# A hybrid attention and recurrence step on one core: pair products for the 32x32 diagonal blocks, the first norm on VectorE, window copies moved

## The chip, the cores and the metric

One core of a Trainium2 chip. The metric is the device time of one execution in microseconds (us). TensorE is PE here, its weight load PEld, VectorE DVE, ScalarE ACT, GpSimd POOL, SyncE SP (it only issues transfers).

## What is computed

One layer of a decoder trunk for a prompt of 2048 tokens and 32 sample tokens (8 sequences of 4): RMSNorm, one wide input projection, a sparse attention branch, a gated linear recurrence (HGRN2) of 4 heads with key and value width 128, merges, output projection, final norm. The recurrence is what the largest edit touches. Within a chunk, G is the running sum of the log gates, and query t takes key s with the factor exp(G[t] - G[s]), for s <= t only:

```python
def step(S, xs):
    qc, kc, vc, gc = xs
    G = jnp.cumsum(gc, axis=2)
    o_inter = jnp.einsum('bhtd,bhde->bhte', qc * jnp.exp(G), S)
    D = jnp.where(tri, G[:, :, :, None, :] - G[:, :, None, :, :], -jnp.inf)
    A = jnp.einsum('bhtd,bhtsd,bhsd->bhts', qc, jnp.exp(D), kc)
    o = o_inter + jnp.einsum('bhts,bhse->bhte', A, vc)
    ...
def rmsnorm(x, g):
    return x * rsqrt(mean(x * x, axis=-1) + EPS) * g
# outputs s_win_k, s_win_v: the sample's window buffers, the oldest 4 rows dropped, 4 new rows behind
```

## The kernel before

The program is written as generators, and the projections are fed as filling work beside the other stages: `load_x` (first norm) and then compression, sample attention, the recurrence (`hgrn`), the bias and setup of the prompt's attention, the prompt phase. A scheduler with a simulated timeline then sets the order in which each engine runs its instructions; it also orders what the engines issue to the DMA queues. So a step that is written in one place may run well before or behind it.

**First norm** (`load_x`, L287 to L326). 17 tiles of up to 128 rows by 1024. Each is loaded (L307, four buffers xt), multiplied by the gain on POOL (L309, xn), squared and summed on ACT (L312), its factor found by DVE in 128x1 steps (L313 to L320), xn scaled on DVE (L321), transposed on PE (L324), and split into a high and a low half (L325 on ACT, L326 on DVE). The projections' weights come in groups: loaded to `wraw` (one buffer, L270), their maximum on DVE (L277), a power-of-two scale (L188 to L193, with a transpose on PE), `us` (L280), and the split into wh (L283, ACT) and wl (L284, DVE). Projection products are L360, L420 and L439.

**Recurrence** (`hgrn`, from L574). 32 units of 256 tokens and one head, each of two pieces of 128 tokens. `factors` prepares one unit ahead: `common` makes G (L637), Bq, Bk, Xo and Kd; then for each level L of 64, 32, 16, 8, 4 the difference to the middle of each block of 2L (DVE, two halves, L679 and L680), its exponential (ACT, L681), and the products with keys and queries (POOL, L682 and L683). Each level so gives the scores between the first and second half of its blocks. `scores` sums them up per piece: a zero product (L697), the blocks of levels 64, 32, 16 into their places (L701), full 128x128 products for levels 8 and 4 (L703) and for pairs within four tokens (L704), each in a plane of a PSUM tile p; DVE then combines them under masks into AT (L706, L708 twice, L709). `values`, one unit later, takes AT and the state S to the outputs (L717 to L736). The 32 sample tokens (`sample_heads`) run beside the later units.

**Window copies** (`keep_windows`, L960 to L966): four DRAM to DRAM transfers of old window rows, written at the end of `sample_attention`. The loads of new window values there are L1179. Gathers of cached pages are issued by POOL (L839).

Of the kernel before, what the change touches and what calls it, by code (L numbers as in the profile page):

```python
# [23 lines left out]
D = 1024  # L24
# [29 lines left out]
def shape_constants():  # L54
# [56 lines left out]
    lm = np.zeros((128, 3, 128), np.float32)  # L111
    s, u = rows[:, None], rows[None, :]
    for i, L in enumerate((8, 4)):
        lm[:, i] = (s // (2 * L) == u // (2 * L)) & (s // L % 2 == 0) & (u // L % 2 == 1)
    lm[:, 2] = (s // 4 == u // 4) & (s <= u)
    c["lmask"] = lm.reshape(128, 384)
# [10 lines left out]
def trunk_kernel(ctx: ExitStack, tc: tile.TileContext, A, O):  # L127
# [120 lines left out]
    def make_projections(s2, st, sb):  # L248
# [38 lines left out]
        def load_x():  # L287
            with tc.tile_pool(name="xa", bufs=2, side="right") as xa, \
# [15 lines left out]
                for i, (t0, r) in enumerate(rows_of):  # L304
# [3 lines left out]
                    xn = xa.tile([128, D], F32, name="xn", bufs=3)  # L308
                    gp.tensor_mul(xn[:r], xt[:r], gB[:r])  # L309
# [11 lines left out]
                    ve.tensor_scalar(xn[:r], xn[:r], y, None, op0=OP.mult)  # L321
# [252 lines left out]
    def hgrn():  # L574
        with ExitStack() as st:
# [4 lines left out]
            lmf = hc.tile([128, 3, 128], F32, name="lmf")  # L580
            sy.dma_start(lmf, A["c_lmask"].rearrange("p (l t) -> p l t", l=3))
            lmi = hc.tile([128, 2, 128], I32, name="lmi")
            ve.tensor_copy(lmi, lmf[:, :2])
            zero = hc.tile([1, 128], BF, name="zero")
            ve.memset(zero, 0.0)
# [81 lines left out]
            def factors(c, h):  # L667
# [19 lines left out]
            def scores(u):  # L687
# [6 lines left out]
                for j in range(NJ):  # L694
                    tj = slice(j * 128, (j + 1) * 128)
                    p4 = pa.tile([128, 4, 128], F32, name="p4")
                    mm(p4[:, 0], zero, zero, True, False)  # L697
                    for li, L in enumerate(LEVELS[:3]):
                        X = u["Xs"][li][:, tj]
                        for s0 in range(0, 128, 2 * L):  # L700
                            mm(p4[s0:s0 + L, 0, s0 + L:s0 + 2 * L], X[:, s0:s0 + L], X[:, s0 + L:s0 + 2 * L], False, True)  # L701
                    for li in (3, 4):
                        mm(p4[:, li - 2], u["Xs"][li][:, tj], u["Xs"][li][:, tj], False, True)  # L703
                    mm(p4[:, 3], u["Bk"][:, tj], u["Bq"][:, tj], False, True)  # L704
                    AT = hp.tile([128, 128], F32, name="AT", bufs=4)
                    ve.tensor_mul(AT, p4[:, 3], lmf[:, 2])  # L706
# [1298 lines left out]
```

## Time and profile before

| | |
|---|---|
| median of 3 runs | 2533.16 us (2530.6 to 2539.71) |
| profiled execution | 2522.99 us |
| its span in the trace | 2521.0 us |
| busy: PE | 2381.2 us, 94% |
| busy: DVE, ACT, POOL | 64%, 45%, 41% |

The span runs from the first to the last instruction. A busy time is the sum of an engine's instruction durations, without overlap; matmuls are pipelined, so a busy PE is not necessarily at its peak. Times in the views below are from the span's start.

### The profile page before, as it was taken

Reading aid. Unit: us, or ns where it says so; the run is one execution under the profiler, and the core shown is the slowest. Engines: PE = TensorE matmul, PEld = TensorE weight load, DVE = VectorE, ACT = ScalarE, POOL = GpSimd, SP = SyncE. Lnnn points to the kernel's source line nnn. Section 1 sums busy time; section 2 is a strip of 40 time slices with the busy share of each in tenths; the row PEclk is TensorE's granted clock in tenths of the full one; section 3 lists DMA queues with packets and bytes.
Section 4 is the critical chain, followed back from the end, with each engine's and each line's share of the span. In section 5 each row is a group of like instructions: output and inputs, shape, how many; then the busy total and the mean of one; then the engine's idle time right before and its main releaser. Section 6 shows DMA issues by size and latency. Waiting matters only on the chain. (4 is left out here: it accounts for less than half of the span.)

```text
span 2521.0 us, 54571 instructions
## 1 busy us (share of the span) xinstructions
PE 2381.2 (94%) x21140; PEld 1589.5 (63%) x21140; DVE 1607.0 (64%) x4325; ACT 1122.3 (45%) x2287; POOL 1022.9 (41%) x1196
## 2 busy tenths in 40 slices
PE   5899999999999999999999879899999999999998
PEld 4788675555785566666666345657666666575765
DVE  8555554656325698777773667667777777867643
ACT  5434323421122344443442345536555656657663
POOL 4200102342111254434550004636566666677864
PEclk9999999999999999999999978999999999999999
DMA  7443315564322433333333552222222222211121
GB/s 275 139 140 112 123 68 164 191 226 153 125 69 100 143 119 115 114 100 109 93 101 96 182 161 65 72 85 72 72 57 74 53 70 55 61 54 44 46 60 45
DMA packets 266709, 264.87 MB, mean 105 GB/s; under 512 B 95101, under 2 KB 237873, under 8 KB 259281
## 3 DMA queue, kind: packets, MB, share of 16 engines
q1 hardware_dynamic: 257936, 223.62, 28.5%
q0 software_dynamic: 8512, 37.75, 4.6%
q8 instruction: 166, 2.72, 0.4%
q14 instruction: 95, 0.77, 0.1%
HBM read 181.90 MB, written 83.55 MB: 105 GB/s over the span
## 5 line engine op out<-in xcount | busy, mean ns | idle before, releaser
L1421 POOL TENSOR_TENSOR Pl<-P,Ph 128x512 f16<-128x512 f32 (+5 forms) x444 | 516.0, 1171 | 419.0 <-ACT Ph L1420 286.7
L1419 ACT ACTIVATE P<-st 128x512 f32<-128x512 f32 (+3 forms) x444 | 264.7, 596 | 207.1 <-PE st L1630 157.8
L360 PEld LDWEIGHTS <-wh 128*128 128x128 f16 x2240 | 214.8, 98 | 177.6 <-issue 28.3
L1420 ACT ACTIVATE Ph<-st 128x512 f16<-128x512 f32 (+5 forms) x444 | 263.3, 595 | 14.8 <-PE po L1428 9.9
L360 PE MATMUL ps<-xh,wh 128*128 128x512 f16 (+1 forms) x1120 | 231.9, 341 | 8.3 <-DVE row L373 8.0
L1508 DVE TENSOR_REDUCE mps<-mx 128x1 f32<-128x512 f32 (+3 forms) x320 | 188.3, 605 | 79.7 <-PE mx L1505 51.2
L360 PE MATMUL ps<-xh,wl 128*128 128x512 f16 (+1 forms) x1120 | 232.4, 340 | 0.0
L360 PE MATMUL ps<-xl,wh 128*128 128x512 f16 (+1 forms) x1120 | 230.3, 340 | 1.4 <-issue 1.4
L439 PE MATMUL ps<-wh,xh 128*128 128x256 f16 (+3 forms) x680 | 189.9, 279 | 5.3 <-ACT xh L325 4.1
L439 PE MATMUL ps<-wh,xl 128*128 128x256 f16 (+3 forms) x680 | 189.4, 278 | 2.1 <-DVE xl L326 2.1
L439 PE MATMUL ps<-wl,xh 128*128 128x256 f16 (+3 forms) x680 | 189.2, 278 | 0.0
L1427 PEld LDWEIGHTS <-Ph 128*128 128x128 f16 (+6 forms) x1776 | 139.2, 98 | 40.0 <-issue 5.0
L360 PEld LDWEIGHTS <-wl 128*128 128x128 f16 x1120 | 108.0, 98 | 85.4 <-issue 8.6
L439 PEld LDWEIGHTS <-xh 128*128 128x128 f16 (+1 forms) x1360 | 130.8, 99 | 29.9 <-issue 5.5
L1428 PEld LDWEIGHTS <-Ph 128*128 128x128 f16 (+6 forms) x1776 | 129.2, 96 | 32.0 <-issue 1.4
L1508 DVE TENSOR_REDUCE mpw<-mx 128x1 f32<-128x512 f32 (+3 forms) x224 | 104.3, 484 | 56.0 <-PE mx L1507 53.6
L682 POOL TENSOR_TENSOR X<-X,kt 128x128 f32<-128x128 f32 x160 | 78.1, 491 | 139.5 <-ACT X L681 139.3
L649 POOL TENSOR_TENSOR Xo<-Xo,qt 128x256 f32<-128x256 f32 x32 | 27.8, 869 | 259.7 <-ACT Xo L648 228.0
L1741 PEld LDWEIGHTS <-xh 128*128 128x128 f16 x1280 | 104.9, 98 | 32.0 <-issue 11.8
L1430 PEld LDWEIGHTS <-Pl 128*128 128x128 f16 (+3 forms) x1776 | 95.6, 97 | 30.8 <-POOL Pl L1421 8.0
L1505 PE MATMUL mx<-kas,qs 96*128 96x512 f16 (+3 forms) x320 | 108.2, 353 | 7.0 <-DVE mps L1508 5.2
L1428 PE MATMUL po<-vs,Ph 128*128 128x64 f16 x1088 | 107.6, 193 | 0.0
(539 smaller groups left out, 5974.8 us busy)
## 6 DMA issues: line engine op xcount, KB each, us to landing
wraw<-in_w_in_dram SPq DMA_DIRECT2D x22, 1024.0 KB
xt<-in_x_prompt_dram SPq DMA_DIRECT2D x32, 512.0 KB
ma_d<-row SPq DMA_DIRECT2D x8, 1040.0 KB
out_y_prompt_dram<-xt SPq DMA_DIRECT2D x16, 512.0 KB
sg<-ma_d SPq DMA_DIRECT2D x56, 128.0 KB
sg<-mb_d SPq DMA_DIRECT2D x56, 128.0 KB
mb_d<-row SPq DMA_DIRECT2D x18, 256.0 KB
q_d<-row SPq DMA_DIRECT2D x4, 1040.0 KB
```

Of the source, the lines that this page charges most:

```text
L360: mm(ps, l[:, kc], xs(r, t0, n)[:, kc], k == 0, k == 23)
L439: mm(ps, xs(l, t0, r)[:, kc], w[:, kc], k == 0, k == 23)
L682: gp.tensor_mul(Xv[:, :, :L], Xv[:, :, :L], kt.rearrange("p (b i) -> p b i", i=2 * L)[:, :, :L])
L1419: ac.activation(P[:n], ps, AF.Exp, scale=1.0 / QS)
L1420: ac.activation(ph[:n], ps, AF.Exp, scale=1.0 / QS)
L1421: sub.tensor_sub(pl[:n], P[:n], ph[:n])
L1427: mm(po[:, r, :w], ph[:n, rs[r]], v[:n, :w], first and r == 0, False)
L1428: mm(po[:, r, :64], ph[:n, rs[r]], v[:n, w:w + 64], False, False)
L1430: mm(po[:, r, :w], pl[:n, rs[r]], v[:n, :w], False, last)
L1505: mm(pmf[:, (x - ka) * 128:(y - ka) * 128], qq[:K, r], kk, i == 0, not sp_)
L1508: ve.tensor_reduce(mp_[:, r, c:c + 1], pmf[:, :n], axis=AX.X, op=OP.max)
L1741: mm(X["ps"], w[:, kc, cs], os_[o][:, kc], k == 0, k == 11)
```

## The change

- Scores: only the 64 pair and the two 32 pairs remain as blocks outside the 32x32 diagonal. The levels 16, 8, 4 and the pairs within four tokens are products of 32x32 for each of the four diagonal blocks. They lie in one 128x128 plane of PSUM, `near`, one 32-wide slot per kind. The zero product is gone.
- AT is one of four fixed tiles, zeroed once. ACT copies the 64 block and the two 32 blocks into it; DVE combines the four kinds in a 128x32 tile `own` (one product, three predicated copies), and one predicated copy over 128x128 puts `own` on the diagonal.
- Factors: one DVE subtraction over both halves, then the absolute value on ACT and the exponential with scale -1.
- First norm: the gain, the factor and the tile in one DVE step, POOL's multiplication is gone.
- The four window copies are issued behind the last load of window values.

```diff
-    for i, L in enumerate((8, 4)):
+    for i, L in enumerate((16, 8, 4)):
...
-    c["lmask"] = lm.reshape(128, 384)
+    own = np.repeat(rows[:, None] // 32 == np.arange(4)[None, :], 32, 1)
+    c["lmask"] = np.concatenate([lm.reshape(128, 128), own], 1).astype(np.float32)
...
-                    xn = xa.tile([128, D], F32, name="xn", bufs=3)
-                    gp.tensor_mul(xn[:r], xt[:r], gB[:r])
...
-                    ve.tensor_scalar(xn[:r], xn[:r], y, None, op0=OP.mult)
+                    xn = xa.tile([128, D], F32, name="xn", bufs=3)
+                    ve.scalar_tensor_tensor(xn[:r], xt[:r], y, gB[:r], op0=OP.mult, op1=OP.mult)
...
+            ATs = []
+            for i in range(4):
+                ATs.append(hc.tile([128, 4, 32], F32, name=f"AT{i}"))
+                ve.memset(ATs[i], 0.0)
...
-                    ref = Gv[:, :, L - 1:L].to_broadcast([128, nb, L])
+                    ref = Gv[:, :, L - 1:L].to_broadcast([128, nb, 2 * L])
...
-                    ve.tensor_tensor(Xv[:, :, :L], ref, Gv[:, :, :L], op=OP.subtract)
-                    ve.tensor_tensor(Xv[:, :, L:], Gv[:, :, L:], ref, op=OP.subtract)
-                    ac.activation(X, X, AF.Exp)
+                    ve.tensor_tensor(Xv, Gv, ref, op=OP.subtract)
+                    ac.activation(X, X, AF.Abs)
+                    ac.activation(X, X, AF.Exp, scale=-1.0)
...
-                    mm(p4[:, 0], zero, zero, True, False)
-                    for li, L in enumerate(LEVELS[:3]):
+                    near = p4[:, 1].rearrange("p (l t) -> p l t", l=4)
+                    for li, L in enumerate(LEVELS[:2]):
                         X = u["Xs"][li][:, tj]
                         for s0 in range(0, 128, 2 * L):
-                            mm(p4[s0:s0 + L, 0, s0 + L:s0 + 2 * L], X[:, s0:s0 + L], X[:, s0 + L:s0 + 2 * L], False, True)
-                    for li in (3, 4):
-                        mm(p4[:, li - 2], u["Xs"][li][:, tj], u["Xs"][li][:, tj], False, True)
-                    mm(p4[:, 3], u["Bk"][:, tj], u["Bq"][:, tj], False, True)
-                    AT = hp.tile([128, 128], F32, name="AT", bufs=4)
-                    ve.tensor_mul(AT, p4[:, 3], lmf[:, 2])
-                    for li in range(2):
-                        ve.copy_predicated(AT, lmi[:, li], p4[:, 1 + li])
-                    ve.tensor_add(AT, AT, p4[:, 0])
+                            mm(p4[s0:s0 + L, 0, s0 + L:s0 + 2 * L], X[:, s0:s0 + L], X[:, s0 + L:s0 + 2 * L], li == 0 or s0 == 64, True)
+                    for li, (l, r) in enumerate([(x, x) for x in u["Xs"][2:]] + [(u["Bk"], u["Bq"])]):
+                        for b in range(4):
+                            bs = slice(j * 128 + 32 * b, j * 128 + 32 * b + 32)
+                            mm(near[32 * b:32 * b + 32, li], l[:, bs], r[:, bs], li == 0 and b == 3, True)
+                    AT = ATs.pop(0)
+                    ATs.append(AT)
+                    ac.activation(AT[:64, 2:], p4[:64, 0, 64:].rearrange("p (b t) -> p b t", t=32), AF.Copy)
+                    for s0 in (0, 64):
+                        ac.activation(AT[s0:s0 + 32, s0 // 32 + 1], p4[s0:s0 + 32, 0, s0 + 32:s0 + 64], AF.Copy)
+                    own = hp.tile([128, 32], F32, name="own")
+                    ve.tensor_mul(own, near[:, 3], lmf[:, 3])
+                    for li in range(3):
+                        ve.copy_predicated(own, lmi[:, li], near[:, li])
+                    ve.copy_predicated(AT, lmi[:, 4:], own[:, None, :].to_broadcast([128, 4, 32]))
...
-                    sy.dma_start(vn, vd[2048 + 16 * gb:2064 + 16 * gb].rearrange("(b t) c -> t b c", t=4))
+                    X_last[0] = sy.dma_start(vn, vd[2048 + 16 * gb:2064 + 16 * gb].rearrange("(b t) c -> t b c", t=4))
...
-            keep_windows()
+            with tc.issue_after(X_last[0].ins):
+                keep_windows()
```

The rows below are engines' instructions in the order in which they run. On PE, the scores of one piece before (p is the PSUM tile, X a level's factors):

```order
L697 LDWEIGHTS zero
L697 MATMUL p_9902<-zero 128x128
L701 MATMUL p_9902<-X_9839 64x64
L701 MATMUL p_9902<-X_9845 32x32 x2
L701 MATMUL p_9902<-X_9851 16x16 x4
L703 MATMUL p_9902<-X_9857 128x128
L703 MATMUL p_9902<-X_9863 128x128
L704 MATMUL p_9902<-Bq,Bk 128x128
```

and with the change:

```order
L706 MATMUL p_9181<-X_9140 64x64
L706 MATMUL p_9181<-X_9146 32x32 x2
L710 MATMUL p_9181<-X_9152 32x32 x4
L710 MATMUL p_9181<-X_9158 32x32 x4
L710 MATMUL p_9181<-X_9164 32x32 x4
L710 MATMUL p_9181<-Bq,Bk 32x32 x4
L706 MATMUL p_9226<-X_9140 64x64
```

The zero product and the three 128x128 products are gone, sixteen products of 32x32 stand in their place, and the second piece follows at once.

On SP, at the start of the program before (the window copies among loads of x and weights):

```order
L966 DMA out_s_win_k_dram<-in_state_win_k_dram 16x4x4064
L307 DMA xt<-in_x_prompt_dram 128x1024
L270 DMA wraw<-in_w_in_dram 128x8x256
L966 DMA out_s_win_k_dram<-in_state_win_k_dram 16x4x4064
L966 DMA out_s_win_v_dram<-in_state_win_v_dram 16x4x4064
L307 DMA xt<-in_x_prompt_dram 128x1024
L966 DMA out_s_win_v_dram<-in_state_win_v_dram 16x4x4064
```

and with the change, in the middle of the program, where the sample attention ends:

```order
L1191 DMA vn<-vw_d 4x4x128
L978 DMA out_s_win_k_dram<-in_state_win_k_dram 16x4x4064 x2
L978 DMA out_s_win_v_dram<-in_state_win_v_dram 16x4x4064 x2
L400 DMA qb_d<-row 128x2080
L272 DMA wraw<-in_w_in_dram 128x8x256
L636 DMA lf<-lf_d 128x256
L637 DMA kt<-kb_d 128x256
```

The four now stand together behind the last load of window values, ahead of a store of projected rows, a weight load and the loads of the recurrence's first units.

## Rows read from the trace of the kernel before

**Rows 1.** The page's first part, busy time, share of the span and instructions.

```profile
PE 2381.2 (94%) x21140; PEld 1589.5 (63%) x21140; DVE 1607.0 (64%) x4325; ACT 1122.3 (45%) x2287; POOL 1022.9 (41%) x1196
```

**Rows 2.** Stretches of the recurrent stage: from and to, length in us, then the busy us and instructions of PE, PEld, DVE, ACT and POOL, the granted clock of PE, the DMA share and GB/s.

```profile
840.00:900.00 60.00, 59.33 (x441) 37.82 (x440) 52.79 (x133) 27.25 (x74) 27.90 (x48) 1.00 0.37 128
...
960.00:1020.00 60.00, 57.91 (x459) 38.83 (x457) 53.73 (x152) 27.31 (x77) 29.23 (x56) 0.99 0.36 119
1020.00:1080.00 60.00, 59.22 (x435) 38.88 (x435) 42.71 (x141) 23.64 (x71) 24.98 (x44) 1.00 0.33 99
...
1260.00:1320.00 60.00, 55.71 (x411) 36.09 (x409) 43.66 (x127) 24.91 (x75) 32.58 (x56) 0.97 0.31 101
```

**Rows 3.** Waits of PE from 840 to 1340 us: what waited, for what; us in total, times, longest us.

```profile
PE pu L781 <- DVE vm L779: 5.4, 3, 3.3
...
PE p L697 <- DVE AT L709: 2.9, 2, 2.5
...
PE pk L690 <- POOL Kd L655: 1.3, 2, 0.9
```

**Rows 4.** PE's timeline at one piece of scores: start us, length us, engine, line, operation, tiles, count.

```profile
928.12 0.23 PE L697 MATMUL p<-zero 1*128 1x128 bf16 x1
928.28 0.55 PE L701 MATMUL p<-X 128*64 128x64 f32 x14
928.76 0.71 PE L703 MATMUL p<-X 128*128 128x128 f32 x4
929.31 0.39 PE L704 MATMUL p<-Bq,Bk 128*128 128x128 f32 x2
929.63 0.23 PE L697 MATMUL p<-zero 1*128 1x128 bf16 x1
```

**Rows 5.** A stretch of L701 alone in the same piece: from and to, length, PE and PEld busy (instructions), clock, DMA share, GB/s.

```profile
928.53:928.66 0.13, 0.13 (x14) 0.13 (x12) 1.00 0.93 323
```

**Rows 6.** Two stretches of L1205 alone (the sample attention's products on four column strips), columns as in rows 5.

```profile
477.86:477.97 0.11, 0.11 (x4) 0.11 (x8) 1.00 0.09 37
477.83:478.65 0.82, 0.81 (x32) 0.81 (x32) 1.00 0.64 200
```

**Rows 7.** Groups of DVE instructions of the recurrence over the whole span: line, operation, tiles, shapes, count, then busy us, mean ns of one, idle us before them and what ended it.

```profile
L680 DVE TENSOR_TENSOR X<-G 128x128 f32<-128x128 f32 x160 | 67.3, 421 | 0.0
...
L679 DVE TENSOR_TENSOR X<-G 128x128 f32<-128x128 f32 x160 | 64.5, 403 | 34.6 <-PE p L701 25.8 <-PE p L703 8.8
...
L708 DVE COPY_PREDICATED AT<-lmi,p 128x128 f32<-128x128 int32 x128 | 34.0, 290 | 0.6
...
L706 DVE TENSOR_TENSOR AT<-p,lmf 128x128 f32<-128x128 f32 x64 | 17.8, 282 | 46.9 <-PE p L704 29.8 <-PE ov L721 17.1
L709 DVE TENSOR_TENSOR AT<-AT,p 128x128 f32<-128x128 f32 x64 | 17.2, 276 | 0.5
...
L652 DVE TENSOR_TENSOR E<-G 128x256 f32<-128x256 f32 x32 | 16.4, 512 | 0.0
```

**Rows 8.** Timeline of DVE, ACT and POOL around the same piece, columns as in rows 4; a length is that of all instructions of the row together (x5).

```profile
929.42 1.63 ACT L681 ACTIVATE X<-X 128x256 f32<-128x256 f32 x5
...
931.69 0.20 ACT L657 ACTIVATE eG<-G 128x2 f32<-128x2 f32 x1
...
931.98 0.17 DVE L751 TENSOR_TENSOR ATs<-pk,lmf 32x32 f32<-32x32 f32 x1
...
932.46 0.45 POOL L682 TENSOR_TENSOR X<-X,kt 128x128 f32<-128x128 f32 x1
```

**Rows 9.** Timeline of the start, columns as in rows 4; in brackets the idle us before it and what ended it.

```profile
9.09 6.95 POOL L309 TENSOR_TENSOR xn<-xt,gB 128x1024 f32<-128x1024 f32 x3 [7.73 <-DMA xt<-in_x_prompt_dram]
...
11.45 2.31 DVE L280 TENSOR_TENSOR us<-wxu,unx 128x1 f32<-128x1 f32 x1
...
13.86 2.19 DVE L320 SCALAR_TENSOR_TENSOR rsx<-rsx,rsz,sx 128x1 f32<-128x1 f32 x1
...
16.17 0.76 DVE L321 TENSOR_SCALAR xn<-xn,rsx 128x1024 f32<-128x1024 f32 x1
...
16.98 0.90 PE L324 MATMUL pt<-ident,xn 128*128 128x128 f32 x3 [5.95 <-DVE xn L321]
```

**Rows 10.** Waits of PE from 0 to 120 us, columns as in rows 3.

```profile
PE tp L183 <- DVE wmx L277: 8.9, 1, 8.9
PE pt L324 <- DVE xn L321: 5.9, 1, 5.9
```

**Rows 11.** Two more groups of DVE over the whole span, columns as in rows 7.

```profile
L1798 DVE SCALAR_TENSOR_TENSOR xt<-xt,rsq,fgB 128x1024 f32<-128x1024 f32 (+1 forms) x17 | 25.4, 1493 | 0.4
...
L326 DVE TENSOR_TENSOR xl<-pt,xh 128x1024 f16<-128x1024 f32 (+1 forms) x17 | 19.7, 1163 | 1.5 <-ACT xh L325 1.5
```

**Rows 12.** SP's queue at the start: start us and how long the issue held it.

```profile
23.41 2.60 SPq L966 DMA_DIRECT2D out_s_win_v_dram<-in_state_win_v_dram  x1
```

**Rows 13.** SP's queue and DVE where the window copies stand with the change, columns as in rows 9.

```profile
593.05 0.28 SPq L1179 DMA_DIRECT2D vn<-vw_d  x1
...
603.88 0.38 SPq L270 DMA_DIRECT2D wraw<-in_w_in_dram  x1
...
609.28 2.29 DVE L277 TENSOR_REDUCE wmx<-wraw 128x1 f32<-128x2048 f32 x1 [1.99 <-DMA wraw<-in_w_in_dram]
```

**Rows 14.** The first stretch of the span, columns as in rows 2.

```profile
0.00:60.00 60.00, 34.60 (x256) 28.22 (x257) 49.47 (x115) 31.61 (x57) 26.88 (x18) 0.97 0.78 270
```

More of the change, by code (lines that the diff above doesn't have):

```diff
@@ L110, in shape_constants @@
     c["edgeq"] = c["edge"].T.copy()
-    lm = np.zeros((128, 3, 128), np.float32)
-    s, u = rows[:, None], rows[None, :]
-    for i, L in enumerate((8, 4)):
+    lm = np.zeros((128, 4, 32), np.float32)
+    s, u = rows[:, None], rows[:, None] // 32 * 32 + np.arange(32)[None, :]
+    for i, L in enumerate((16, 8, 4)):
         lm[:, i] = (s // (2 * L) == u // (2 * L)) & (s // L % 2 == 0) & (u // L % 2 == 1)
-    lm[:, 2] = (s // 4 == u // 4) & (s <= u)
-    c["lmask"] = lm.reshape(128, 384)
+    lm[:, 3] = (s // 4 == u // 4) & (s <= u)
+    own = np.repeat(rows[:, None] // 32 == np.arange(4)[None, :], 32, 1)
+    c["lmask"] = np.concatenate([lm.reshape(128, 128), own], 1).astype(np.float32)
     rst = np.ones(2048, np.float32)
@@ L579, in hgrn @@
             po = st.enter_context(tc.tile_pool(name="hpo", bufs=1, space=PSUM, side="right"))
[L580 to L585, printed above, removed]
+            lmf = hc.tile([128, 8, 32], F32, name="lmf")
+            sy.dma_start(lmf, A["c_lmask"].rearrange("p (l t) -> p l t", l=8))
+            lmi = hc.tile([128, 8, 32], I32, name="lmi")
+            ve.tensor_copy(lmi, lmf)
+            ATs = []
+            for i in range(4):
+                ATs.append(hc.tile([128, 4, 32], F32, name=f"AT{i}"))
+                ve.memset(ATs[i], 0.0)
             rst = hc.tile([128, 256], F32, name="rst")
@@ L696, in scores @@
                     p4 = pa.tile([128, 4, 128], F32, name="p4")
[L697 to L698 removed]
+                    near = p4[:, 1].rearrange("p (l t) -> p l t", l=4)
+                    for li, L in enumerate(LEVELS[:2]):
                         X = u["Xs"][li][:, tj]
                         for s0 in range(0, 128, 2 * L):
[L701 to L709 removed]
+                            mm(p4[s0:s0 + L, 0, s0 + L:s0 + 2 * L], X[:, s0:s0 + L], X[:, s0 + L:s0 + 2 * L], li == 0 or s0 == 64, True)
[13 more added lines that the diff above has]
+                    ve.copy_predicated(AT, lmi[:, 4:], own[:, None, :].to_broadcast([128, 4, 32]))
+                    AT = AT.rearrange("p b t -> p (b t)")
                     u["AT"].append(AT)
@@ L750, in sample_heads @@
                     AT = hp.tile([32, 32], F32, name="ATs")
-                    ve.tensor_mul(AT, pb[:32, :32], lmf[:32, 2, :32])
+                    ve.tensor_mul(AT, pb[:32, :32], lmf[:32, 3])
                     yield
@@ L1218, in outputs @@
                                pT[:64, :128].rearrange("p (b h t) -> p h b t", h=8, t=4))
-            Xs = [{}, {}]
+            Xs, X_last = [{}, {}], [None]
             for _ in zip(compressed(0, Xs[0]), compressed(1, Xs[1])):
```

## The prediction, made before the changed kernel ran

> **What bounds the kernel now.** First the busy times of the whole span: TensorE (PE) is busy 2381.2 of 2521.0 us, 94% [rows 1], so time can come only from PE's work or from its idle rest of some 140 us. Next the stretches of the recurrent stage, where the largest edit lies: PE is busy 58 to 59 of each 60 us up to 1080 and still 55.7 near the end. VectorE (DVE) has 53 to 54 of 60 in the first third of the stage and 43 later; ScalarE (ACT) 24 to 27; GpSimd (POOL) 25 to 33 [rows 2]. Then PE's waits there: in 500 us the largest group is 5.4 us in three waits, the finished scores AT held PE for 2.9 and POOL's Kd for 1.3 [rows 3]. So little feeds PE too late there; a microsecond taken from PE's own instructions in this stage is a microsecond of the end, as long as the feeders keep up.
>
> **Scores, what is removed.** The timeline of one 128-token piece: the zero product starts at 928.12, the next piece's zero product at 929.63, so a piece costs PE 1.50 us. Of this the 64, 32 and 16 level blocks (L701) run to 928.76, and three full 128x128 products (L703 twice, L704) take from there to about 929.6 [rows 4].
>
> **Scores, what comes in.** One 64x64 pair stays: L701's first stretch, from 928.28 to where its small blocks begin, 0.26 us [rows 4, 5]. Behind it come two 32x32 pairs and four kinds of four 32x32 blocks, 18 products, 36 matmuls as f32 counts them, on four column strips of 32. What does one of these cost? Two rows bear on it. The four-strip product of the sample attention (L1205) starts four matmuls of 128 columns in 0.11 us, and 32 of them last 0.82 us [rows 6]: 26 ns a matmul of 128 columns, so the four strips work side by side. With 32 columns in place of 128, a round of four is 0.11 x 32/128 = 0.027 us; 36 matmuls in ten rounds are 0.27 us. And L701's own small blocks, on strips too, are 12 of the 14 matmuls in the 0.13 us behind the pair, 11 ns each [rows 5], which for 36 gives 0.40. With the 64 pair and an allowance of 0.10 for the change of tile sizes a piece is 0.63 by the one and 0.76 by the other; I take 0.70 between them, since both rows are near in kind and neither has these tiles. Saved: 0.80 us x 64 pieces = **51 us**. Ends: 0.63 gives 56, 0.76 gives 47; and were each 32-column matmul to cost the 26 ns of L1205's mean, a piece would be 0.26 + 0.94 + 0.10 = 1.30 and the gain 13 (rival 1).
>
> **What the scores and factors ask of the feeders.** DVE per unit (two pieces; 32 units): ten halves of 128x128 at 0.40 to 0.42 become five of 128x256 at 0.51 (L652's form), which saves 1.5 us; the evacuation per piece was 0.28 + 2 x 0.29 + 0.28 = 1.14 [rows 7] and becomes four of 128x32, priced at the 0.17 of a 32x32 product [rows 8], and one predicated 128x128 at 0.29: 0.97. So DVE loses 1.9 us a unit, 60 in all. ACT gets a second activation at each level, 160 x 0.33 = 53 us (five exponentials in 1.63 us), and six copies a unit, 192 x 0.20 = 38 us, at the price of a small one [rows 8]: 91 us over some 500, which takes it from 25 of 60 to about 36. That is free only as cover by PE's work and ACT's idle time; without the cover it is rival 3. POOL's products stay, 0.45 each [rows 8]. With a tenth less PE time in the stage, DVE's 53.5 of 60 in 840 to 1020 would be full [rows 2], were it not for the 1.9 us a unit that it loses. I take back a third of the 16 us that this third of the stage saves: **+5** (0 to +25).
>
> **First norm.** At the start POOL multiplies three tiles by the gain, 6.95 us for three, before DVE can scale the first; the first transposes begin at 16.98 after a wait of 5.95 us. Meanwhile DVE's 128x1 steps take 2.31 and 2.19 us [rows 9], where a 32x32 step takes 0.17 elsewhere [rows 8]: they stand beside POOL's multiplication. Without it I take these two at 0.2 each, 4.1 us earlier. Against that the fused step costs more than the old scaling. Its nearest row is the final norm's same operation, 1.49 us on average [rows 11], against 0.76 [rows 9]; in an undisturbed place I take 1.2, the 1.16 of a two-operand step of that size [rows 11], so +0.44. The transposes would begin near 13.3. In the first 120 us PE waits 8.9 us once for the weight maximum and 5.9 in one wait for the first norm [rows 10]; the second is what shrinks. I take **-5** for the start, with some for the later tiles. Ends: -14, if the 8.9 goes down with it by as much, and +3, if the fused step is 0.7 dearer and the scaling of four tiles stands on the path. What is late next is the weight maximum.
>
> **Windows.** Four copies of 1016 KB leave the start, where the longest of the four issues holds the queue for 2.60 us [rows 12] and the memory is at 270 GB/s [rows 14], and are issued behind the last load of window values (593.05). Next on that queue stands a weight load, at 603.88, whose reduction already waited 1.99 us for it [rows 13]. The four move 4.1 MB, at 270 GB/s [rows 14] 15 us of all DMA engines. If the weights came 15 us later, DVE would stand still at the reduction and with it the evictions behind it. The weight buffer is single, but weights are loaded and split ahead of their use, which leaves PE with work. I take **+2** (0 to +6, at worst 15), and no more gain at the start than counted, as no first wait of PE there ends on a transfer [rows 10].
>
> **Sum.** -51 + 5 - 5 + 2 = -49. The profiled execution took 2522.99 us (span 2521.0), so 2474 on its scale. The median of the runs shown, 2533.16, is 10 above; on that scale **2484**. This case's own range: 2468 to 2500 (all ends together 2463 to 2519).
>
> **Rivals.**
> 1. *The 32x32 products run one after another*, 26 ns each: -13 - 5 + 2, and nothing given back: **2517**. For it: L1205's mean is 26 ns, and nothing there shows that fewer columns would make it less. Against it: 11 ns each in L701 [rows 5, 6]. Chance 0.10. The Trainium skill has this as a rule: "TensorE: Matmul & The Clock Gate", section "Wait — 56ns, not 53.3ns?", says that starts of consecutive matmuls are never nearer than about 25 ns, however few the columns. L701's stretch disagrees with it for products on different strips; by the rule a piece would be 1.30 and the kernel this rival.
> 2. *The evacuation paces the stage.* DVE at 53.5 of 60 has no room for a faster PE in the first third [rows 2], and the shorter pieces ask for their evacuations closer together; half of the 51 comes back as waits for AT and for the projections' evictions: -26 - 5 + 2, **2505**. Against it: DVE gets 60 us less to do, it is at 43 later, and PE waited for AT only 2.9 us [rows 2, 3]. Chance 0.12. The Trainium skill warns of this in "TensorEngine Tiling (Array Packing)", section "PSUM Bottleneck": after array packing the copy out of PSUM can become the limit and both engines should share it, which this change does in part.
> 3. *Slower: the unit's own chain becomes what PE waits for.* Subtract, Abs, exponential, product follow one another level by level, and five Abs at 0.33 and six copies at 0.20 lengthen it by 2.85 us a unit. If ACT holds the levels back, PE stands at the scores, the 51 saved lies idle, and 32 x 2.85 = 91 is added: 2533 + 91 - 3 = **2621**. It decides as soon as POOL's last product of a unit comes less than 2.85 us ahead of its scores. Against it: units are prepared ahead, PE's waits for POOL there are 1.3 us [rows 3], and POOL at 0.9 a level is slower than ACT at 0.66 [rows 8], so that POOL paces the levels anyway. Chance 0.04.
>
> That the whole order of work moves, so that something outside these places eats the rest (ends near no change), gets 0.06.
>
> **How the numbers follow.** The forecast has 0.68. A measurement of this kernel tells about 0.5%, 12.7 us, from no change, so faster means below 2520.5. The forecast, rival 2, and six tenths of rival 1 lie there: 0.68 + 0.12 + 0.06 and a point of the remainder, 0.87. Within 0.5%: the rest of rival 1 and most of the remainder, 0.08. Slower: rival 3 and a point, 0.05. The range, 2460 to 2517, holds the forecast but for its tails (0.63), rival 2 (0.12) and about half of rival 1 (0.05).
>
> **What the profile of the changed kernel would show.** A piece between two 64x64 pairs in PE's timeline at 0.65 to 0.75 us (1.3 would be rival 1). PE still busy 56 or more of each 60 us in the recurrent stage, and its last values product 45 to 50 us earlier than before (far more waits for AT: rival 2; waits for POOL's X or ACT at the scores: rival 3). First transposes near 13 us, and the 128x1 steps of DVE there under 0.3 us. The window copies near 590 us and the next weight reduction later by at most their 15 us, with few us of PE idle behind it. The prediction is wrong if the pieces are short but PE's idle in the stage has grown by as much.

## The result, and the profile after

The changed kernel takes **2499.28 us** (median of 4 runs, 2497.57 to 2502.58), the kernel before 2534.85 beside it: a ratio of 0.9859, 95% interval 0.9838 to 0.988, or 36 us. Forecast were 2484, 49 us less than before, in a range of 2460 to 2517.

The first line of its page: PE is as full as before, with 1088 matmuls more.

```profile
PE 2357.9 (94%) x22228; PEld 1554.0 (62%) x22228; DVE 1575.8 (63%) x4232; ACT 1198.0 (48%) x2639; POOL 989.9 (40%) x1179
```

To say where the time went, the span is cut at two places that both kernels have: the first product of the recurrent stage's scores on PE (the transposes of Kd), and the first product of the prompt phase (L1620 before, L1633 after). Rows are as in [rows 2]: from and to, length, PE busy and so on. Before:

```profile
0.00:627.90 627.90, 580.66 (x4318) 406.63 (x4319) 367.12 (x830) 233.87 (x367) 140.67 (x125) 0.99 0.49 159
627.90:1493.80 865.90, 828.32 (x5898) 536.26 (x5896) 546.43 (x1545) 303.87 (x775) 257.59 (x455) 0.98 0.36 115
1493.80:2511.10 1017.30, 972.26 (x10928) 646.63 (x10926) 689.01 (x1938) 583.82 (x1145) 624.66 (x618) 0.97 0.23 63
```

and after:

```profile
0.00:628.70 628.70, 586.54 (x4339) 408.37 (x4340) 359.71 (x843) 240.31 (x387) 106.42 (x118) 0.99 0.49 160
628.70:1469.80 841.10, 798.04 (x6965) 498.67 (x6963) 519.86 (x1437) 371.68 (x1105) 258.13 (x445) 0.97 0.37 117
1469.80:2486.10 1016.30, 973.33 (x10927) 646.96 (x10926) 691.74 (x1938) 585.32 (x1146) 625.35 (x618) 0.97 0.23 64
```

The whole difference of the two traces, 25 us, lies in the middle stretch: 865.9 to 841.1. There PE's busy time fell by 30 us, and what it stood idle (length less busy) grew from 37.6 to 43.1. The median differs by 11 us more than the traces, and the granted clock shows why: the profiled execution of before ran at a mean of 0.980, its timed runs at 0.971 to 0.979 (one of 2543.12 us at 0.971, one of 2525.1 at 0.978), the changed kernel's at 0.973 to 0.976. So the trace of before shows an execution some 12 us shorter than the median; in which stretch those 12 us would lie is not known.

**The scores.** PE's timeline of two unbroken pieces after:

```profile
859.11 0.48 PE L706 MATMUL p<-X 128*64 128x64 f32 x4
859.39 0.23 PE L710 MATMUL p<-X 128*32 128x32 f32 x2
859.42 0.20 PE L706 MATMUL p<-X 128*32 128x32 f32 x2
859.44 0.34 PE L710 MATMUL p<-X 128*32 128x32 f32 x20
...
859.64 0.26 PE L710 MATMUL p<-Bq,Bk 128*32 128x32 f32 x7
859.83 0.48 PE L706 MATMUL p<-X 128*64 128x64 f32 x4
...
860.54 0.71 PE L729 MATMUL pu<-v,kd 128*128 128x128 f32 x4
```

A piece is 0.72 us (859.11 to 859.83), where [rows 4] had 1.50: 20 matmuls of 32 columns begin between 859.44 and 859.60.

**The waits of PE** in the middle stretch of the changed kernel (us, times, longest):

```profile
PE pu L793 <- DVE own L717: 6.0, 3, 2.6
PE ov L614 <- DVE o_sb L611: 5.3, 5, 1.6
PE ps L421 <- ACT piece L426: 5.0, 3, 2.5
PE ps L361 <- DVE row L383: 4.8, 3, 3.8
PE pk L694 <- POOL Kd L658: 3.7, 4, 2.0
...
PE p L710 <- POOL X L687: 1.1, 3, 0.6
```

Three of the five largest, 16 us, end on VectorE, each of another line, which points at its queue more than at one operation. For the finished factors (POOL's X, the last row) PE waits 1.1 us only. In 840 to 960 VectorE has 54.5 and 54.4 of 60, as full as in [rows 2] although a unit asks some 1 us less of it; that PE now asks sooner would explain it:

```profile
840.00:900.00 60.00, 54.06 (x559) 33.28 (x559) 54.52 (x138) 35.95 (x118) 33.46 (x56) 0.97 0.38 127
900.00:960.00 60.00, 57.17 (x630) 35.48 (x628) 54.39 (x147) 35.77 (x126) 34.43 (x59) 1.00 0.42 137
```

**The clock behind a wait.** The longest of the waits at L793, and the stretch around it (rows as in [rows 2]):

```profile
1077.52 1.19 PE L793 MATMUL pu<-vm,kd_s 32*128 32x512 f32 x1 [2.61 <-DVE own L717]
```

```profile
1066.80:1077.00 10.20, 8.11 (x108) 4.19 (x105) 8.70 (x27) 8.11 (x32) 8.15 (x16) 1.00 0.51 172
1077.00:1083.90 6.90, 6.38 (x13) 2.13 (x14) 3.79 (x19) 0.94 (x6) 3.18 (x8) 0.51 0.33 99
1083.90:1090.00 6.10, 6.10 (x99) 3.42 (x96) 1.05 (x5) 1.91 (x9) 0.04 (x1) 1.00 0.40 110
```

PE waited 2.61 us, and then the granted clock was 0.51, that is 1.2 GHz, for 6.9 us: the wait cost itself and some 3 us more. Such stretches add to 27.1 us in the middle stretch of before and to 44.6 after. In the recurrent stage of the changed kernel there are seven, each beginning within 4 us of a wait of 1.2 to 3.8 us; four other waits of 1.4 to 1.8 us brought none. The 17.5 us more of slow clock in the middle stretch are 9 us of PE's work.

### The profile page after: what moved, and what is told of

It reads as the page before. It is cut to its first block, busy times and chain, and to the rows that moved or that the text cites. A ratio compares the mean times of both kernels' runs of the same rounds, so it can differ in the third digit from the quotient of the medians.

```text
span 2496.1 us, 57172 instructions
## 1 busy us (share of the span) xinstructions
PE 2357.9 (94%) x22228; PEld 1554.0 (62%) x22228; DVE 1575.8 (63%) x4232; ACT 1198.0 (48%) x2639; POOL 989.9 (40%) x1179
## 4 chain that ended last, share of the span: by engine, by line
PE 68%; DVE 14%; DMA 7%; ACT 4%; issue 4%; POOL 1%; SPq 1%; DVEq 0%; ACTq 0%; POOLq 0%
PE ps L361 14%; PE ps L440 9%; PE ps L1786 7%; PE ps L1754 6%; PE ps L421 4%; PE st L1643 3%; PE st L1633 3%; PE mx L1518 3%; DVE X L683 2%; DMA wraw<-in_w_in_dram 2%; PE ph L920 2%; PE po L1440 2%; PE po L1443 2%; PE po L1441 2%; DVE mps L1521 1%
## 5 line engine op out<-in xcount | busy, mean ns | idle before, releaser
L361 PE MATMUL ps<-xl,wh 128*128 128x512 f16 (+1 forms) x1120 | 236.0, 347 | 1.1 <-issue 1.0
L1440 PEld LDWEIGHTS <-Ph 128*128 128x128 f16 (+5 forms) x1776 | 138.8, 98 | 41.3 <-issue 6.9
L1441 PEld LDWEIGHTS <-Ph 128*128 128x128 f16 (+5 forms) x1776 | 128.7, 96 | 32.7 <-issue 1.4
L1521 DVE TENSOR_REDUCE mpw<-mx 128x1 f32<-128x512 f32 (+3 forms) x224 | 104.9, 485 | 49.6 <-PE mx L1520 46.7
L652 POOL TENSOR_TENSOR Xo<-Xo,qt 128x256 f32<-128x256 f32 x32 | 30.5, 953 | 260.4 <-ACT Xo L651 229.3
L1518 PE MATMUL mx<-kas,qs 96*128 96x512 f16 (+3 forms) x320 | 109.8, 355 | 10.4 <-DVE mps L1521 7.7
L1440 PE MATMUL po<-vs,Ph 128*128 128x65 f16 x1088 | 106.6, 192 | 0.8 <-DVE otmp L1535 0.8
```

Source lines behind the costliest of these rows:

```text
L361: mm(ps, l[:, kc], xs(r, t0, n)[:, kc], k == 0, k == 23)
L1440: mm(po[:, r, :w], ph[:n, rs[r]], v[:n, :w], first and r == 0, False)
L1441: mm(po[:, r, :64], ph[:n, rs[r]], v[:n, w:w + 64], False, False)
L1518: mm(pmf[:, (x - ka) * 128:(y - ka) * 128], qq[:K, r], kk, i == 0, not sp_)
L1521: ve.tensor_reduce(mp_[:, r, c:c + 1], pmf[:, :n], axis=AX.X, op=OP.max)
```

## Experiments

Each was timed in several rounds against the kernel before on the same chip, which took a median of 2532.61 to 2535.96 us there. The three stretches are cut as above, one trace for each kernel; idle is PE's, and slow is the sum of the stretches at half clock, both of the profiled execution.

| kernel | median us | ratio to before [95%] | first stretch | middle: length, idle, slow | prompt: length, idle, slow |
|---|---|---|---|---|---|
| before | 2534.85 | 1 | 627.9 | 865.9, 37.6, 27.1 | 1017.3, 45.0, 51.4 |
| the change | 2499.28 | 0.9859 [0.9838, 0.988] | 628.7 | 841.1, 43.1, 44.6 | 1016.3, 43.0, 64.6 |
| scores_only | 2503.71 | 0.987 [0.9847, 0.9893] | 623.2 | 844.7, 42.0, 58.0 | 1025.8, 47.0, 51.2 |
| factors_only | 2506.67 | 0.9893 [0.987, 0.9917] | 628.9 | 849.7, 21.5, 24.7 | 1016.7, 42.1, 50.4 |
| norm_only | 2536.07 | 1.0009 [0.9993, 1.0025] | 621.3 | 872.5, 41.7, 35.0 | 1032.8, 52.6, 70.9 |
| windows_only | 2539.7 | 1.0025 [1.0011, 1.0039] | 638.2 | 859.1, 35.8, 29.3 | 1026.5, 48.4, 59.4 |
| products_twice | 2491.1 | 0.9825 [0.9806, 0.9844] | 624.9 | 833.6, 29.4, 23.9 | 1020.6, 42.8, 37.5 |
| vm_pool | 2514.88 | 0.9922 [0.9901, 0.9942] | 625.1 | 841.6, 47.2, 44.8 | 1035.1, 55.2, 74.7 |
| halves_exp | 2504.5 | 0.9882 [0.9863, 0.9901] | 625.8 | 845.6, 43.1, 61.4 | 1023.1, 47.3, 54.6 |
| windows_early | 2517.92 | 0.9938 [0.992, 0.9955] | 619.7 | 860.1, 50.1, 64.4 | 1027.6, 52.4, 68.7 |
| last_level_first | 2489.53 | 0.983 [0.9806, 0.9854] | 621.5 | 835.1, 39.8, 42.1 | 1015.1, 43.3, 46.7 |
| scores_factors | 2527.2 | 0.9975 [0.9961, 0.9988] | 620.0 | 849.4, 47.1, 43.8 | 1041.3, 55.5, 89.3 |
| no_subtract | 2467.28 | 0.9737 [0.9712, 0.9763] | 633.7 | 806.3, 29.0, 44.4 | 1026.2, 43.0, 51.2 |
| less_vector | 2470.93 | 0.9754 [0.9729, 0.978] | 616.3 | 828.7, 30.5, 34.1 | 1023.5, 44.6, 51.2 |

### One part at a time

The first four take one part of the change each into the kernel before; the edit is that part of the diff, so it is not shown again.

**scores_only.** 

> Only the scores and their masks change; factors, first norm and windows are as before. Theory A (the scores are the whole gain of the stage, what is lost of it goes to waits of PE on VectorE and to the clock behind them): ratio 0.987 to 0.990, 25 to 33 us faster, the two pieces of a unit in 1.4 to 1.6 us where nothing stands between them, PE waits of 840 to 1340 above the 18.8 us of before. Theory B (the sum of the prediction holds and the run-to-run spread hides it): 0.980 to 0.983, over 43 us faster. Theory C (the gain needs the shorter VectorE work of the factors as well): under 15 us.

Measured 0.987, 32 us: Theory A, at its edge, and by its signs too: two pieces with nothing between them take 1.41 to 1.48 us, and PE's waits from 840 to 1340 are 29.3 us. PE's products of the scores, counted as under products_twice below, fall from 99.1 us to 57.1.

**norm_only.** 

> Only the first norm changes. Theory A: first transposes 3.5 us earlier, of which 2 to 4 us arrive at the end: ratio 0.998 to 0.999. Rival: the later tiles' waits take it back, 1.000 +- 0.001.

Measured 1.0009 with 1 inside the interval: the rival. The first transposes came 3.9 us earlier (13.04), but the first product of the compression, behind all tiles of x, came 0.8 us later than before. The first stretch as a whole ends 6.6 us sooner with the same 4318 matmuls, but it differs by as much between kernels that share this part of the program, and the stretches behind it are 22 us longer.

**windows_only.** 

> Only the four window copies move. Theory A: the weight reduction behind them waits 2 us longer, PE waits near 600 us 0 to 3 us more, nothing is won at the start: ratio 0.999 to 1.002. Rival: the start's loads come earlier and PE's waits of the first 120 us shrink by some us: 0.997 to 0.999.

Measured 1.0025, 6 us slower, above Theory A's range (the interval reaches into it). The first stretch is 10 us longer, the middle one 7 shorter. DVE's weight reduction behind the copies waited 4.09 us for its weights, [rows 13] having 1.99.

**factors_only.** 

> Only the factors change: one subtraction, Abs, exponential. Theory A: VectorE gets about 1.5 us a unit less to do by the prediction, but the subtraction's mean in the changed kernel is 631 ns where 512 were assumed and PE is the bound: ratio 0.998 to 1.002. Rival (VectorE paces the first third of the stage): 0.994 to 0.997. Rival 3 of the prediction (Abs lengthens the chain): above 1.003.

Measured 0.9893, 27 us faster: the rival, and more than it asked for. Not one product was taken from PE. Its middle stretch shows what changed: PE busy is the 828 us of before, in 16 us less.

```profile
628.90:1478.60 849.70, 828.19 (x5900) 534.03 (x5898) 525.38 (x1392) 348.89 (x931) 266.03 (x456) 0.99 0.37 118
```

The idle time fell from 37.6 to 21.5, PE's waits on VectorE in this stretch from 21.0 to 5.6, VectorE's busy time by 21. So in the kernel before VectorE held PE back, by a few late arrivals that were read as too little to matter; one trace on each side shows it, and the order of work moved as well. By their ratios the four parts add to -33 - 27 + 2 + 6 = -52 us, and together they give 36.

The granted clocks of the timed runs say where most of the 16 us between lie. One minus the granted clock, times the span, estimates what half clock cost a run (too much where PE had nothing to do in it). On average it is 49 us in factors_only, where the kernel before had 65 beside it; 61 in scores_only, 67 in norm_only, 71 in windows_only; 64 in the change, where the kernel before had 63. So the clock is 13 us of the parts' 52 and nothing of the change's 36. Without it the parts add to 38 and the change gives 36: what is lost when the parts stand together is mostly clock.

### Both large parts, and what each of the others is worth beside them

**scores_factors.** Without the first norm's and the windows' part.

> Scores and factors change, the first norm and the window copies stay as before. Theory A (the parts add, less what scores and factors both take from the same waits): 2495 to 2503 as the changed kernel, since norm and windows are worth 0 and +6: ratio 0.983 to 0.988. Rival (norm or windows are worth something beside the others): above 0.990, as the changed kernel with early windows was.

Measured 0.9975: the rival, and 24 us slower than scores_only, from which it differs by the factors alone. Alone the factors gave 27 us; beside the scores they give nothing. Their middle stretches, scores_only first:

```profile
623.20:1467.90 844.70, 802.68 (x6950) 500.18 (x6947) 541.80 (x1615) 332.47 (x965) 272.84 (x456) 0.97 0.37 118
620.00:1469.40 849.40, 802.31 (x6989) 502.09 (x6987) 520.89 (x1448) 371.41 (x1116) 268.06 (x458) 0.97 0.36 115
```

VectorE has 21 us less to do, as in factors_only, but PE's idle time is 5 us longer, and its waits on VectorE are 27.1 us against 22.3. By the estimate above 16 of the 24 us are clock.

Against the changed kernel, scores_factors reaches the prompt phase at 1469.4 us, the changed kernel at 1469.8. What it loses, it loses behind that, in a program that none of the parts touches:

```profile
1469.40:2510.70 1041.30, 985.78 (x10928) 652.81 (x10926) 695.31 (x1945) 588.52 (x1150) 628.51 (x618) 0.96 0.23 64
```

against 1016.3 in the changed kernel's third row above. PE runs the same products there in another order; that the scheduler starts the phase from another state would explain it. PE's idle time is 12.5 us longer (its waits for the maxima mps are 16 us against 9, for the loads of oah 8.4 against 4.7) and the slow clock 24.7 us, 12 us of work; the two make up the 25 us. In the table the same phase runs from 1015 to 1041 us.

**windows_early.** `keep_windows()` without `issue_after`, as before.

> The changed kernel, with the window copies issued where they were before. Moved alone they cost 0.25 per cent. Theory A (they delay the weights behind them): 3 to 7 us faster than the changed kernel, 2492 to 2496. Rival (their cost depends on the rest of the order and is chance): within 2 us or slower.

Measured 0.9938, 19 us slower than the change: the rival. Moved alone, the copies cost 6 us, beside the other parts they seem to win 19, but in the traces 11 us of that are the prompt phase and 19 the middle stretch, most of them idle and slow clock, while the first stretch is 9 shorter. What the move itself is worth can't be told from that. With the first norm as it was besides, the kernel is scores_factors: its first stretch is 620.0 us against 619.7 here, so the first norm gives nothing at its own place beside the other parts either.

### Where the gain of the scores goes

**products_twice.**

```diff
+                    twice = p4[:, 2].rearrange("p (l t) -> p l t", l=4)
...
+                    for li, (l, r) in enumerate([(x, x) for x in u["Xs"][2:]] + [(u["Bk"], u["Bq"])]):
+                        for b in range(4):
+                            bs = slice(j * 128 + 32 * b, j * 128 + 32 * b + 32)
+                            mm(twice[32 * b:32 * b + 32, li], l[:, bs], r[:, bs], False, True)
```

> The changed kernel, with the 32x32 products of every piece computed a second time into a spare plane of the same PSUM tile; 2048 matmuls more, nobody reads them. Theory A (a 32x32 matmul costs PE 11 to 14 ns beside its neighbours, as the unbroken pieces of 0.72 to 0.77 us show, and PE's own work sets most of the stage): 15 to 30 us slower than the changed kernel, 2514 to 2530. Theory B (each costs about 25 ns in this mix, so the pieces were too dear and that is where the forecast gain went): 45 us or more slower, 2545 or above. Theory C (feeders pace the stage, PE has idle time to spare): under 8 us slower.

Measured 2491.1, 8 us **faster** than the change: no theory had that sign. PE's time in score products, counted from each group's first start to the start of the next other product and without waits, is 57.0 us in the change and 78.4 here: 21.4 us for 2048 matmuls, 10.4 ns each. So Theory B falls, and Theory A's price holds or is a little high. But the idle of the middle stretch fell by 13.7 us and the slow clock by 20.7 (10 us of work):

```profile
624.90:1458.50 833.60, 804.15 (x8941) 510.17 (x8940) 504.59 (x1464) 373.88 (x1114) 263.33 (x451) 0.99 0.38 121
```

Useless work does not feed PE. What changed is the order: the scheduler, told of longer scores, put other work between, and PE's waits of over 1 us went from 19 to 9. The timed runs show the same: the granted clock is 0.980 to 0.983 where the change has 0.973 to 0.976, some 17 us by the estimate above, so that without the clock this kernel is the slower one by 8. VectorE's unchanged program also took 15 us less in the middle stretch, its 160 subtractions 85 us in place of 101; why is taken up under the factors below. That the order alone did all this was not tried apart from the added work.

**vm_pool.**

```diff
-                            ve.tensor_scalar(vm[:, b], v, bd[:, 4 * b2 + b:4 * b2 + b + 1], None, op0=OP.mult)
+                            gp.tensor_scalar(vm[:, b], v, bd[:, 4 * b2 + b:4 * b2 + b + 1], None, op0=OP.mult)
```

> The changed kernel, with the 32 small masked products of the sample tokens (vm) on POOL in place of VectorE. Theory A (waits of PE on VectorE's queue, and the 1.2 GHz stretches that follow each of them, take back the gain): PE's three waits at L793 behind VectorE's own (6.0 us) go, with the three slow stretches behind them (13.7 us at half speed): 6 to 12 us faster than the changed kernel, 2487 to 2493. Rival (the time lost there is lost elsewhere anyway): within 3 us.

Measured 0.9922, 16 us slower, which neither theory had. The waits at L793 went, and VectorE's same queue held PE at the next place instead:

```profile
PE p L706 <- DVE own L719: 6.2, 4, 2.1
```

The middle stretch is as long as the change's (841.6); in the traces the prompt phase is 19 us longer (1035.1 to 1016.3), with its products again in another order.

**halves_exp.**

```diff
-                    ac.activation(X, X, AF.Abs)
-                    ac.activation(X, X, AF.Exp, scale=-1.0)
+                    ac.activation(Xv[:, :, :L], Xv[:, :, :L], AF.Exp, scale=-1.0)
+                    ac.activation(Xv[:, :, L:], Xv[:, :, L:], AF.Exp)
```

> The changed kernel, without Abs: the exponential runs on the two halves of a level apart, with scale -1 and +1 (160 activations of 128x256 become 160 more of 128x128). Theory A (VectorE's queue is what PE waits for, ScalarE has room): ScalarE 15 to 30 us less busy, time within 4 us of the changed kernel. Rival (the longer chain over ScalarE is what holds the scores back): 8 us or more faster.

Measured 5 us slower than the change, just outside Theory A's 4, with intervals that overlap; ScalarE 28 us less busy in the middle stretch, the idle there the same 43.1 us. Less work for ScalarE gives nothing here.

**last_level_first.** The products of the level 4 come first, then the pairs, 8, 16, and the 64 and 32 blocks last.

```diff
+                    kinds = list(enumerate([(x, x) for x in u["Xs"][2:]] + [(u["Bk"], u["Bq"])]))
+                    for li, (l, r) in [kinds[2], kinds[3], kinds[1], kinds[0]]:
...
+                            mm(near[32 * b:32 * b + 32, li], l[:, bs], r[:, bs], li == 2, True)
...
+                            mm(p4[s0:s0 + L, 0, s0 + L:s0 + 2 * L], X[:, s0:s0 + L], X[:, s0 + L:s0 + 2 * L], False, True)
```

> The changed kernel, with each piece's products in another order: the level whose factors come last stands first, so that once a piece begins, all it needs is there; PE's order then has the score products in 94 unbroken groups instead of 117. Theory A (a break costs a group some 0.1 to 0.2 us, and that is why PE saved 39 us in the stage and not the 51 of unbroken pieces): PE's score time without waits falls from 57 us by 3 to 5, 0 to 6 us faster. Rival (chance of the order, as in the four runs before): anything within 15 us either way, with idle and slow-clock time of the stage to match and PE's net work unchanged.

Measured 2489.53, 10 us faster, but not by the score products: their time without waits is 61.0 us, not 57.0 less 3 to 5. In the change, groups of at most 20 matmuls hold 546 of the 2432 and cost 12.6 us more than they would in unbroken pieces; here that is 7.7 us, as expected, and the longer groups, with the 64 block last, give 9 back. In the traces 7 us lie in the first stretch, which the edit does not touch, 6 in the middle (3 of them idle) and 1 in the prompt phase. That fits the rival's chance of the order, but for PE's score time, which rose.

**no_subtract.**

```diff
-                    ve.tensor_tensor(Xv, Gv, ref, op=OP.subtract)
-                    ac.activation(X, X, AF.Abs)
+                    ac.activation(X, G, AF.Abs)
```

> The changed kernel, with the five subtractions of a unit left out: ScalarE takes the absolute value of G itself. This leaves out part of the computation of the factors; 160 VectorE steps of 0.63 us, 101 us in all, are gone. Theory A (PE's waits in the stage, and the slow clock behind them, come from VectorE's queue): idle from the stage's first scores to the prompt phase falls from 43 to under 25 us, slow-clock stretches from 45 to under 25: 15 to 30 us faster than the changed kernel. Rival (waits move to the next feeder or are chance of the order): within 8 us.

Measured 2467.28, 32 us faster than the change, slightly beyond Theory A, whose two signs it misses: idle fell to 29.0, not under 25, and the slow clock stayed at 44.4. VectorE is busy 440.5 us in the middle stretch where the change has 519.9:

```profile
633.70:1440.00 806.30, 777.33 (x6842) 488.73 (x6843) 440.48 (x1301) 368.35 (x1110) 246.15 (x436) 0.97 0.38 120
```

By medians this is worth nearly what the whole change is. In the traces it is 20 us, and PE's idle time in the three stretches makes up nearly all of it (128.3 us in the change, 108.9 here). The prompt phase begins 29.8 us earlier, but 123 matmuls fewer lie in the middle stretch, and 50 and 73 more before and behind it. The step left out also makes each level's chain shorter; PE's waits for the end of that chain were 1.1 us in the change (POOL's X), so VectorE's time is the likelier cause. The order moved here too, and products_twice, with nothing left out, has 29.4 us of idle in its middle stretch.

**less_vector.** On last_level_first, two VectorE steps a unit less, with nothing left out:

```diff
-                ve.tensor_tensor(E2.rearrange("p (b i) -> p b i", i=L), GL[:, :, L - 1:L].to_broadcast([128, n // L, L]), GL, op=OP.subtract)
-                ac.activation(Kd, E2, AF.Exp)
+                if n == NC:
+                    for b in range(0, n, L):
+                        ac.activation(Kd[:, b:b + L], G[:, b:b + L], AF.Exp, bias=G[:, b + L - 1:b + L], scale=-1.0)
...
+                    if L == 64:
+                        nref = hp.tile([128, nb], F32, name="nref")
+                        ve.tensor_scalar(nref, Gv[:, :, L - 1], -1.0, None, op0=OP.mult)
+                        for b in range(nb):
+                            ac.activation(Xv[:, b, :L], Gv[:, b, :L], AF.Exp, bias=Gv[:, b, L - 1:L], scale=-1.0)
+                            ac.activation(Xv[:, b, L:], Gv[:, b, L:], AF.Exp, bias=nref[:, b:b + 1])
```

> A version from what the runs showed: last_level_first, and two VectorE steps of a unit less. Kd takes its difference in the exponential itself (bias, scale -1) and so does the level of 64, with one 128x2 step for the negative reference; the other four levels are as in the change. About 1.0 us of VectorE a unit goes, 31 us in all, a third of what no_subtract took away. Theory A (VectorE's queue holds PE back in the stage): 5 to 12 us faster than last_level_first, 2478 to 2485, with less idle than its 39.8 us up to the prompt phase. Rival (the order that the scheduler finds decides, above all in the prompt phase, whose program is the same): the time up to the prompt phase shorter or equal, but the whole anywhere from 2475 to 2510.

Measured **2470.93**, 0.9754 of before [0.9729, 0.978]: 19 us faster than last_level_first (whose interval lies apart), more than Theory A's 5 to 12 and below the rival's range, 28 faster than the change, the fastest kernel with the whole computation. Idle in its middle stretch is 30.5 us against 39.8:

```profile
616.30:1445.00 828.70, 798.21 (x6951) 501.27 (x6949) 502.82 (x1433) 393.86 (x1217) 280.39 (x461) 0.98 0.37 120
```

ScalarE took 18 us more on itself there, without harm. In the traces the middle stretch shows 6 and the first 5, and the prompt phase is 8 longer; but the profiled execution is less_vector's slowest (2480.27) and last_level_first's fastest (2483.63). In the timed runs the granted clock is 0.979 to 0.982 against 0.972 to 0.978, by the estimate above 12 of the 19 us. PE's waits on VectorE fell by 2.4 us in the middle stretch (20.9 to 18.5), those on ScalarE and on transfers by 7.3. So the version is faster; that the freer queue of VectorE made it so is not shown.

## Why the prediction was right or wrong

**Right: what bounds, and the piece.** A piece was forecast at 0.70 us, 0.65 to 0.75 on sight, and is 0.72. Rival 1 is out: doubled, the products cost 10.4 ns each, nearer to the 11 of [rows 5] than to 26. The rule of the Trainium skill that stood beside it ("TensorE: Matmul & The Clock Gate", section "Wait — 56ns, not 53.3ns?", never under about 25 ns from start to start) doesn't hold in this trace for products that go to four column strips in turn: 20 started in 0.16 us.

Two of its signs failed. PE was to be busy 56 or more of each 60 us: from 840 to 1320 three of eight such stretches have less (54.1, 55.8, 53.4); and 58 to 59 up to 1080 was read without 900 to 960, which had 57.2 before the change. The last values product was to come 45 to 50 us earlier and comes 10.5 earlier (1342.7 against 1353.2); another 13.5 us less lie between it and the prompt phase, with 52 projection products fewer there (586 against 638): part of what the scores free was filled with products that stood behind.

**Mis-sized: the term of 51 us.** PE's score products took 99.1 us without waits before and 57.0 after, so 42 were saved. Sixty-four unbroken pieces of 0.72 would be 46. The forecast multiplied an unbroken piece by 64; in the order as run the pieces lie in 119 groups among other products. Those of at most 20 matmuls cost 12.6 us more than in unbroken pieces, the longer ones 1.6 less: together the 11 us.

**Wrong for the kernel before: the factors at no gain.** "So little feeds PE too late there" led to costing VectorE's relief by its cover alone. factors_only gave 27 us without touching PE's work. [rows 3] were read by their largest groups: together PE's waits there are 18.7 us, 17 of them on VectorE, and in factors_only 5.9; the clock adds to it, 16 of the 27 us in the timed runs. Beside the scores the same edit gave nothing (scores_factors against scores_only), so for the changed kernel a gain of the factors is not shown either way. The size was off as well: VectorE was to lose 1.9 us a unit; the subtraction takes 0.64 us there instead of 0.51, and the copy onto AT's diagonal 0.38 instead of 0.29 (840 to 1340 us):

```profile
L683 DVE TENSOR_TENSOR X<-G 128x256 f32<-128x256 f32 x140 | 81.4, 638 | 0.0
...
L720 DVE COPY_PREDICATED AT<-lmi,own 128x128 f32<-128x128 int32 x60 | 22.0, 379 | 1.2
```

so that a unit loses about 1.0 (ten halves 4.1 to five of 0.64, and an evacuation that stays at 1.12 a piece). Both prices were averages over two cases. In the changed kernel's trace the 33 subtractions with hardly any work of POOL beside them took 0.41 to 0.43 us, the 91 with POOL busy nearly all along 0.73 on average; before, the halves of L680 took 0.28 and 0.54. In products_twice only 49 of the 160 had POOL beside them all along, which is where its 16 us of shorter subtractions come from. That POOL's work is the cause was not tried by a run.

**Mis-sized: the 5 given back.** In the traces it is 5.5 us of idle and 9 of clock. The measured 2499 lies between the forecast's 2484 and rival 2's 2505, nearer to the rival: PE waits on VectorE 28.4 us in the middle stretch, 21.0 before, though for its whole queue rather than for the evacuation alone. The Trainium skill's warning ("TensorEngine Tiling (Array Packing)", section "PSUM Bottleneck") is borne out by this trace only in so far as the copies out of PSUM are part of that queue: for their own plane of PSUM (L706 behind own) PE waits 0.9 us. Moving the blocks' copies to ScalarE, as it advises, did leave ScalarE with room (36 of 60). How far VectorE paces the stage stays open: no_subtract and less_vector, which relieve it, were faster, scores_factors and vm_pool, which do too, were not.

**The first norm: right at its place, nothing at the end.** The first transposes were forecast near 13.3:

```profile
13.39 1.97 PE L325 MATMUL pt<-ident,xn 128*128 128x128 f32 x8 [2.59 <-DVE xn L322]
```

VectorE's small steps beside POOL fell as expected (the step of 2.19 us in [rows 9] takes 0.21 here, the fused one 1.28 where 1.2 were taken):

```profile
11.58 0.21 DVE L320 SCALAR_TENSOR_TENSOR rsx<-rsx,rsz,sx 128x1 f32<-128x1 f32 x1
...
12.05 1.28 DVE L322 SCALAR_TENSOR_TENSOR xn<-xt,rsx,gB 128x1024 f32<-128x1024 f32 x1
```

but norm_only measures no gain; the next waits take it (the compression begins no sooner), and -5 should have been 0.

**The windows: alone the sign is right, and the size at the edge of its range.** The weight reduction waits 7.14 us where [rows 13] had 1.99:

```profile
588.59 1.70 SPq L978 DMA_DIRECT2D out_s_win_k_dram<-in_state_win_k_dram  x2
...
601.60 0.40 SPq L272 DMA_DIRECT2D wraw<-in_w_in_dram  x1
...
611.04 2.29 DVE L279 TENSOR_REDUCE wmx<-wraw 128x1 f32<-128x2048 f32 x1 [7.14 <-DMA wraw<-in_w_in_dram]
```

and moved alone they cost 6 us where 2 were taken and 0 to 6 allowed. Beside the other parts no cost shows (windows_early).

**Missing: the order.** The remaining chance of 0.06 for "the whole order of work moves" was far too small as a source of size: the untouched prompt phase alone differs by up to 26 us between these kernels. How much of the 36 us is owed to the order that this change happened to get stays open; with the same two large parts the measured gain went from 6 us (scores_factors) to 36. What holds throughout is PE's saving of some 42 us in the scores; what relieving VectorE is worth changes with the order.

**The number.** That 2499 lies in the range is in part luck. The scores fell 9 us short of their term, the first norm gave none of its 5, the windows alone cost 4 more, and some 9 more than the 5 taken came back as waits and slow clock; against that stand the factors, left at nothing, with 27 us where they were changed alone. These sizes come from different kernels and do not add up to the 36.

## What to carry to other kernels

An engine that is busy 58 of 60 us may still be paced by the next one: add up its waits by the engine that ends them, not by line, and count the slow clock behind each. When a PE edit makes the stage shorter, price the feeders' queues at the new length, and measure the relief of a feeder beside that edit and not only alone: here it gave 27 us alone and none beside the scores. Where a scheduler sets the order, an edit of 1% is within what a new order elsewhere gives or takes: cut the span at common places and compare the stretches before crediting the edit.

## What was not expected of the hardware

Within one kernel the time follows the mean granted clock: before, 2543.12 us at 0.971 and 2528.07 at 0.977. A wait of 2.61 us of PE was followed by 6.9 us at 1.2 GHz, and in the changed kernel's recurrent stage no slow stretch began without such a wait within 4 us before it. VectorE's subtraction of one shape took 0.41 to 0.96 us, 0.63 on average; with hardly any work of POOL beside it 0.41 to 0.43, with POOL busy nearly all along 0.73 on average.
